# Another order of the wide stage's pairs, another list of PSUM banks, and the weights' quarters one pair later

## The chip, the cores and the metric

The kernel runs on one core of a Trainium2 chip. The metric is device time in microseconds (us). A core has a matrix engine (PE, with its weight load PEld), a vector engine (DVE), a scalar engine (ACT), a third elementwise engine (POOL) and SP, which here only issues transfers (DMAs). Every engine takes its own queue of instructions in order. A matmul writes to PSUM, eight banks of 128x512 fp32; DVE and ACT read PSUM and write on-chip memory. Engines wait for each other on semaphores.

## The reference

One layer of a trunk with two branches, for one sequence of 1024 rows of 1024, in fp32, with the RMS norm of the stream behind it:

```python
h = rms_norm(x, norm_w) * (1 + scale) + shift
gm_u, gm_v, gm_z, ssm_z, xbc, dt_raw, g_a, g_b = split(h @ w_in)
y_a = spatial_gating(gelu(gm_u), gelu(gm_v), ...) * silu(gm_z)      # W_s applied to layer_norm(v)
xbc = silu(causal_depthwise_conv(xbc, conv_w, conv_b))               # 4 taps
xs, bm, cm = split(xbc)
y_b = rms_norm((ssd_scan(xs, dt, a, bm, cm) + xs * d_skip) * silu(ssm_z))   # by groups
merged = sigmoid(g_a) * (y_a @ w_proj_a) + sigmoid(g_b) * (y_b @ w_proj_b)
return rms_norm(x + gate * (merged @ w_out), final_norm_w)
```

The product `h @ w_in` has 1024 x 1024 times 1024 x about 11,000; it is the "wide stage" of the kernel.

## The kernel before, in words

**Numbers.** fp32 values are split in a high and a low part (names end in `h` and `l`), and each product is made of three matmuls per tile: high x high, high x low, low x high.

**The wide stage.** The columns of `w_in` go in 41 pairs of two 128-column blocks. A pair is one call of `pair` (L594 on): seven products p1, p5, p6, p3, p2, p7, p4 of a Strassen-like scheme, each `product` (L580 on) being 12 matmuls of 128x512 into one bank (L588). The operands from the activations (`b11`, `t1` and so on) are made once; those from the weights are sums and differences of four loaded blocks `a11 a21 a22 a12` (DVE, L575 to L578), split into high parts by ACT (L536) and low parts by DVE (L537). The banks of a pair are `px` (p1, then p6 on top of it, later p7 and p4), and banks for p5 with p3 and for p2. In the profile these banks appear as `xNAME`, `yNAME`, `zNAME`, where NAME is the kind of pair: `cb` and `x` for the two kinds of convolution pairs, `uz` for a gated pair of z_g and u, `z`, `g` for the light ones, `v` for the first four. The evacuations stand in line L604: `c1NAME` is the first half of the pair's result and starts with ACT's copy of p1 before p6 is added to the same bank. So **p6 of a pair cannot start before ACT has copied p1**.

**What follows a pair.** A convolution pair has two results, each handled by `conv_done` (L912 on): ACT scales (L914), three DVE operations add the other taps (L916), ACT applies the silu (L918), and the result is stored to `s_d`. A light pair only needs ACT and a store. A gated pair g needs `mix(g)` (16 matmuls of 128x128 with the gating weights, then DVE), which reads `vn`, the normalized v; eight ACT operations (L879) write it once the statistics `vr` of v are there (L871) and v is loaded back as `vm`.

**Order of the work.** `jobs` (L934 to L961) is a list of pairs; the driver loop (L1316 on) makes the weights of pair n+1 while pair n runs. After each product `run_tasks()` issues what `later(delay, f)` has put `delay` products ahead: the statistics, `mix_load` and `mix` are placed so. From pair `NPRE` on, when the early pool `gx` is closed, the projection weights `w_proj_b` are prepared in 32 quarters, one every 4.3 products (`wb_quarter`, L820 on), and stored to `wb_d`. The instruction order of PE is as written; on ACT, DVE, POOL and SP a scheduler orders the instructions when the kernel is built.

**After the wide stage** come the SSD groups (`sl`, `dcy`, `yi`, `sp` and so on), with the first output projection `pma` between them. PSUM banks are handed out from a free list here (`bank` and `release`, L486 to L497) whose first order is `BANKS` (L146). Then the second projection is made by the same seven-product scheme (`multiply`, L1576 on, matmuls at L1584): its product p1 runs eight steps, the first of which writes the four banks `x0` to `x3`, which `places_of` (L1667) maps to physical banks. A bank is free once its last reader is done. In the last two groups of the SSD the row sums are in banks `pq6_1` and `pq7_1`; DVE copies them to the tiles `cwt` and `tri`, whose old content is no longer used.

Of the kernel before, what the change touches and what calls it, by code (L numbers as in the profile page):

```python
# [21 lines left out]
NG = 8  # L22
# [13 lines left out]
def hybrid_kernel(  # L36
# [24 lines left out]
    x, out = x[0], out[0]  # L61
# [42 lines left out]
    def store(dst, src):  # L104
        A.dma_start(dst, src)
# [37 lines left out]

    hpool = tc.tile_pool(name="hpool", bufs=1, reuse_waits="tile")
    hp = hpool.__enter__()
    BANKS = (1, 4, 3, 0, 2, 7, 5, 6)  # L146
    BN = ("b11", "t1", "t2", "b22", "t3", "b21", "t4")
    bop = {}
    for nm in BN:
# [26 lines left out]
    def wide(name, dt=F32):  # L176
        return w4[0].tile([P, S], dt, name=name, tag="w4", bufs=w4[1])
# [321 lines left out]
    def numbered(pool, c):  # L499
        for b in range(8):  # L500
            pool.tile([P, 512], F32, name=f"{c}{b}_0", tag=f"{c}{b}")
# [4 lines left out]
    def later(delay, f, *a):  # L506
        tasks.append((slot[0] + delay, f, a))

    def run_tasks():
        slot[0] += 1  # L510
        due = [t for t in tasks if t[0] <= slot[0]]
        for t in due:
            tasks.remove(t)
            t[1](*t[2])
# [79 lines left out]
    def pair(name, ops, done1, done2, after=None, whole=False):  # L594

        keep = pin if name in first_c1 and not p2r else lambda i: i
        after = after or (lambda n: None)  # L600

        def out(f, *a):
            with tc.high_priority():
                keep(f(*a))  # L604

        def p2():
            pz = bank(f"z{name}")
            product(pz, ops["p2"], "b21")
            out(V.tensor_add, c1[:, 0:512], c1[:, 0:512], pz)

        px = psum.tile([P, 512], F32, name=f"x{name}", tag="px", bufs=2)
        product(px, ops["p1"], "b11")
        c1 = first_c1.pop(name) if name in first_c1 else wide(f"c1{name}")
        out(A.copy, c1[:, 0:512], px)
        after(0)
        py = bank(f"y{name}")
        product(py, ops["p5"], "t1")
        c2 = wide(f"c2{name}") if p2r else None
        p5 = c2[:, 512:1024] if p2r else gm.tile([P, 512], F32, name=f"p5{name}", tag="p5")
        out(A.copy, p5, py)  # L620
        after(1)
        if pending:
            pending.pop()()
        product(px, ops["p6"], "t2", False)
        out(A.copy, c1[:, 512:1024], px)
        after(2)
        product(py, ops["p3"], "b22", False)
        out(V.tensor_add, c1[:, 512:1024], c1[:, 512:1024], py)
        after(3)
        if not whole:  # L630
            p2()
            after(4)
            done1(c1)
        product(px, ops["p7"], "t3", False)
        c2 = c2 or wide(f"c2{name}")
        out(V.tensor_add, c2[:, 512:1024], p5, px)
        after(4 if whole else 5)
        if whole:
            p2()
            done1(c1)  # L640

        def p4():
            product(px, ops["p4"], "t4", False)
            out(A.copy, c2[:, 0:512], px)
            done2(c2)

        if whole:
            p4()
        else:
            pending.append(p4)  # L650
# [156 lines left out]
    def wb_load(i):  # L807

        k, j = quarters[i]
        wbr[i] = raw = pre.tile([P, 4, P], F32, name=f"wbr{i}", tag="wbr", bufs=2)  # L810
        for k0, t in ((k, raw[:, 0:4:3]), (k + KT, raw[:, 1:3])):
            load(t, w_proj_b[k0 * P : (k0 + 1) * P, :].rearrange("p (b j c) -> p j b c", b=2, j=4)[:, j])
# [84 lines left out]
    def zg_done(g):  # L897
        def done(cz):
            A.activation(cz, cz, AF.Silu)
            V.tensor_mul(vns[g], cz, vns[g])  # L900
        return done

    def u_done(g):
        def done(cu):
            A.activation(cu, cu, AF.Gelu_apprx_tanh)
            V.tensor_mul(cu, cu, vns[g])
            store(ya_d[g], cu)
        return done
# [19 lines left out]
    def gate_done(i):  # L928
        def done(cg):
            A.activation(cg, cg, AF.Tanh, scale=0.5)  # L930
            store(th_d[i * P : (i + 1) * P, :], cg)
        return done

    def gcol(i):  # L934
        return (COL_GA if i < 8 else COL_GB) + (i % 8) * P

    jobs = []
    for g in range(0, NG, 2):
        jobs.append((f"v{g}", COL_V + g * P, COL_V + (g + 1) * P, v_done(g), v_done(g + 1), None))
    convs = []  # L940
# [5 lines left out]
    light = []  # L946
    for g in range(NG):
        light.append((f"z{g}", COL_Z + 2 * g * P, COL_Z + (2 * g + 1) * P, z_done(g, 0), z_done(g, 1), None))
    gpairs = []
    for i in range(2, 16, 2):  # L950
        gpairs.append((f"g{i}", gcol(i), gcol(i + 1), gate_done(i), gate_done(i + 1), None))
    for g in range(NG):
        jobs.append(convs.pop(0))
        jobs.append((f"uz{g}", COL_ZG + g * P, COL_U + g * P, zg_done(g), u_done(g), g))
    light = [p for q in zip(light, gpairs[:5] + [None] * 3) for p in q if p]
    while convs:
        jobs.append(convs.pop(0))
        for _ in range(1 if len(convs) in (1, 4, 7) else 2):
            jobs.append(light.pop(0))
    tail = gpairs[5:]  # L960


# [245 lines left out]
    def start_ssd():  # L1208
        fetch(2)
        done_d[0] = 2  # L1210
# [91 lines left out]
    def with_last(n, d):  # L1302
        def done(t):
            d(t)
            beside(n)
        return done

    todo = jobs + tail
    seconds, fold = [], []
    NPRE = 20  # L1310
    pre = None
    ops = pair_weights(*todo[0][:3], pinned=True)
    ps0.__exit__(None, None, None)
# [3 lines left out]
    for n, (name, _, _, d1, d2, g) in enumerate(todo):  # L1317
        if n == 4:
            later(7, stats)
        if n == NPRE:  # L1320
            gxpool.__exit__(None, None, None)
            prepool = tc.tile_pool(name="prepool", bufs=1, side="right", reuse_waits="tile")
            pre = prepool.__enter__()

            fold.append(pre.tile([P, NH], F32, name="fold", tag="fold"))
            wb_load(0)
            for i in range(len(quarters)):
                later(2 + 43 * i // 10, wb_quarter, i)
        if n == len(jobs):
            while tasks:  # L1330
                run_tasks()
            prepool.__exit__(None, None, None)
            gmpool.__exit__(None, None, None)
            w4pool.__exit__(None, None, None)
            p2rpool = tc.tile_pool(name="p2r", bufs=1, side="right", reuse_waits="tile")
            p2r = p2rpool.__enter__()
            w4[:] = [p2r, 4]
            first_c1[name] = wide(f"c1{name}")
        if 0 < n < len(todo) - 1:
            nxt = pair_weights(*todo[n + 1][:3])  # L1340
        if n + 2 == len(todo):
            wspool.__exit__(None, None, None)
            p2xpool = tc.tile_pool(name="p2x", bufs=1, side="right", reuse_waits="tile")
            p2x = p2xpool.__enter__()
            start_ssd()
        if g is not None:
            later(1 if g else 4, mix, g)
            if g + 1 < NG:
                later(7, mix_load, g + 1)
        if n + 1 == len(todo):  # L1350
            hand[0] = True
            pair(name, ops, with_last(5, d1), with_last(6, d2), beside, True)
        else:
            pair(name, ops, d1, d2, ops.get("after"), n in (3, len(jobs) - 1))
        ops = nxt if n else seconds[0]
# [56 lines left out]
    numbered(psum, "k")  # L1412
    free.extend(BANKS)
    for k in (6, 7):
# [249 lines left out]
    ps3 = tc.tile_pool(name="ps3", bufs=1, space=PSUM, reuse_waits="tile")  # L1664
    psb = ps3.__enter__()
    numbered(psb, "q")
    places_of = {"x": (1, 2, 3, 0), "y": range(4, 8)}  # L1667
    assert all(b > 3 for b in free[6:])
    wo, wor = {}, {}
    KO = (4, 5, 6, 7, 0, 1, 2, 3)  # L1670
# [90 lines left out]
    def inv_root(sq):  # L1761

        y, t, v = sq[:, 2:3], sq[:, 3:4], sq[:, 1:2]
        V.tensor_scalar(t, sq[:, 0:1], 1.0 / D, EPS, op0=ALU.mult, op1=ALU.add)
        V.tensor_scalar(y.bitcast(I32), t.bitcast(I32), -0.5, float(0x5F3759DF), op0=ALU.mult, op1=ALU.add)
        V.tensor_scalar_mul(v, t, -0.5)
        for _ in range(3):
            V.scalar_tensor_tensor(t, y, y, v, op0=ALU.mult, op1=ALU.mult)
            V.scalar_tensor_tensor(y, t, 1.5, y, op0=ALU.add, op1=ALU.mult)
        return y  # L1770
# [24 lines left out]
    for n, t in enumerate(tiles):  # L1795
# [22 lines left out]
        if last:  # L1818
            V.scalar_tensor_tensor(sq[:, 0:1], part[:, 0:1], part[:, 1:2], part[:, 2:3], op0=ALU.add, op1=ALU.add)
            y = inv_root(sq)  # L1820
# [4 lines left out]
        else:  # L1825
            V.tensor_add(r, pw, xr)
            A.activation(xr, r, AF.Square, accum_out=sq[:, 0:1])  # L1827
            y = inv_root(sq)
# [35 lines left out]
```

## Time and profile before

| | us |
|---|---|
| median of 3 runs | 1406.11 (1402.32 to 1409.07) |
| the profiled execution | 1407.12 |
| its span, first to last instruction | 1405.4 |
| mean granted clock of PE | 0.995 of full speed |
| wide stage, first `cb` product to last `g` pair's first product | 155.84 to 892.01 |
| second projection, first product | from 1155.61 |

The profiled execution lies 1.0 us above the median; about 1.7 us of it lie outside the span. The views used are the busy time of each engine, the list of waits (engine, what it was to compute, for whom it waited: us in total, times, longest), busy times by stretches of time, and the timeline, whose rows are start, duration, engine, line, operation, output and inputs, and at the end in brackets how long the engine was idle before, and what ended that.

### The profile page before, as it was taken

Reading aid. Unit: us, or ns where it says so; the run is one execution under the profiler, and the core shown is the slowest. Engines: PE = TensorE matmul, PEld = TensorE weight load, DVE = VectorE, ACT = ScalarE, POOL = GpSimd, SP = SyncE. Lnnn points to the kernel's source line nnn. Section 1 sums busy time; section 2 is a strip of 40 time slices with the busy share of each in tenths; the row PEclk is TensorE's granted clock in tenths of the full one; section 3 lists DMA queues with packets and bytes.
Section 4 is the critical chain, followed back from the end, with each engine's and each line's share of the span. In section 5 each row is a group of like instructions: output and inputs, shape, how many; then the busy total and the mean of one; then the engine's idle time right before and its main releaser. Section 6 shows DMA issues by size and latency. Waiting matters only on the chain.

```text
span 1405.4 us, 20414 instructions
## 1 busy us (share of the span) xinstructions
PE 1373.7 (98%) x7015; PEld 1132.1 (81%) x7015; DVE 1040.0 (74%) x1827; ACT 771.4 (55%) x1422; POOL 209.0 (15%) x198
## 2 busy tenths in 40 slices
PE   8999979999999999999999999999999999999997
PEld 6677868888888888888888888888888878888786
DVE  4677777667766898688788887478888768686743
ACT  6663466656666565555566555477786734233401
POOL 0000000000000000001010000017898870000000
PEclk9999989999999999999999999999999999999999
DMA  8555623332343576767676865488898849977432
GB/s 266 156 164 161 184 90 106 106 113 83 104 121 112 159 212 204 227 204 236 193 232 206 255 212 166 165 320 300 293 316 299 276 136 320 408 255 259 135 120 75
DMA packets 272043, 279.23 MB, mean 199 GB/s; under 512 B 18972, under 2 KB 224196, under 8 KB 271940
## 3 DMA queue, kind: packets, MB, share of 16 engines
q1 hardware_dynamic: 197956, 210.16, 47.8%
q10 hardware_dynamic: 73984, 67.78, 14.1%
q8 instruction: 55, 0.90, 0.3%
q14 instruction: 48, 0.39, 0.1%
HBM read 194.58 MB, written 83.30 MB: 198 GB/s over the span
## 4 chain that ended last, share of the span: by engine, by line
PE 80%; DVE 6%; DMA 6%; ACT 3%; issue 2%; SPq 2%; POOL 1%; POOLq 0%; ACTq 0%; DVEq 0%
PE xx L588 6%; PE xz L588 6%; PE xuz L588 6%; PE xg L588 5%; PE xcb L588 5%; PE pma L91 5%; PE yp L1584 5%; PE po L91 4%; PE x L1584 4%; PE yx L588 3%; PE yz L588 3%; PE yuz L588 3%; PE yg L588 3%; PE ycb L588 3%; PE yi L91 2%
## 5 line engine op out<-in xcount | busy, mean ns | idle before, releaser
L799 POOL TENSOR_TENSOR wog<-wog,gb 128x1024 f32<-128x1024 f32 x8 | 20.4, 2545 | 729.1 <-DVE wbr L835 535.5
L56 ACT ACTIVATE dcy<-dcy,nacs 128x128 f32<-128x128 f32 x256 | 78.4, 388 | 16.9 <-POOL dcy L56 16.4
L56 POOL TENSOR_SCALAR_AFFINE_SELECT dcy<-dcy 128x1024 f32<-128x1024 f32 x32 | 37.0, 1155 | 103.6 <-ACT ea L56 103.3
L918 ACT ACTIVATE ac<-ac 128x1024 f32<-128x1024 f32 x32 | 33.9, 1061 | 23.5 <-DVE ac L916 23.3
L56 ACT ACTIVATE ea<-dcy 64x512 f32<-64x512 f32 x64 | 40.3, 630 | 5.4 <-DMA dcy<-acs_d 5.0
L91 PE MATMUL pma<-yh,wah 128*128 128x512 f32 x128 | 43.0, 417 | 0.0
L91 PE MATMUL pma<-yh,wal 128*128 128x512 f32 x128 | 42.6, 414 | 0.0
L56 POOL TENSOR_TENSOR yz<-y,sl 128x512 f32<-128x512 f32 x32 | 41.3, 1291 | 0.6
L56 DVE TENSOR_TENSOR dcy<-dcy,pc 128x1024 f32<-128x1024 f32 x32 | 38.9, 1217 | 2.7 <-PE pc L94 1.8
L56 DVE TENSOR_TENSOR ym<-yn,ea 128x512 f32<-128x512 f32 (+1 forms) x32 | 19.9, 621 | 28.3 <-PE yn L91 28.1
L916 DVE SCALAR_TENSOR_TENSOR ac<-c2cb,cwt,ac 128x1023 f32<-128x1023 f32 (+2 forms) x24 | 30.6, 1275 | 13.1 <-ACT ac L914 12.9
L91 PE MATMUL pma<-yl,wah 128*128 128x512 f32 x128 | 39.9, 393 | 0.0
L56 POOL TENSOR_TENSOR y<-y,ym 128x512 f32<-128x512 f32 (+1 forms) x32 | 36.6, 1145 | 14.2 <-DVE ym L56 14.1
L916 DVE SCALAR_TENSOR_TENSOR ac<-c2x,cwt,ac 128x1023 f32<-128x1023 f32 (+2 forms) x24 | 31.8, 1325 | 8.6 <-ACT ac L914 7.1
L91 PE MATMUL yi<-dcy,xd 128*64 128x128 f32 x512 | 35.0, 279 | 3.2 <-DVE xe L56 2.9
L1827 ACT ACTIVATE xr<-r 128x1024 f32<-128x1024 f32 x7 | 7.4, 1061 | 53.2 <-issue 39.0
L1817 POOL TENSOR_TENSOR r<-r,fnw 128x256 f32<-128x256 f32 (+1 forms) x3 | 2.7, 916 | 220.5 <-ACT xr L1816 220.5
L91 PEld LDWEIGHTS yi<-dcy,xd 128*64 128x64 f32 x512 | 27.3, 136 | 9.5 <-issue 4.2
L91 PE MATMUL sp<-xe,bn 128*128 128x256 f32 x112 | 32.7, 409 | 0.0
L56 DVE SCALAR_TENSOR_TENSOR yn<-yn,par,rb 128x512 f32<-128x512 f32 x32 | 24.5, 766 | 9.6 <-DMA yn<-yb_d 9.6
L916 DVE SCALAR_TENSOR_TENSOR ac<-c1cb,cwt,ac 128x1023 f32<-128x1023 f32 (+2 forms) x24 | 30.6, 1277 | 0.7 <-ACT ac L914 0.7
L916 DVE SCALAR_TENSOR_TENSOR ac<-c1x,cwt,ac 128x1023 f32<-128x1023 f32 (+2 forms) x24 | 30.6, 1276 | 0.0
(2834 smaller groups left out, 4341.2 us busy)
## 6 DMA issues: line engine op xcount, KB each, us to landing
sl<-s_d SPq DMA_DIRECT2D x32, 768.0 KB
s_d<-ac ACTq DMA_DIRECT2D x32, 512.0 KB
dcy<-acs_d SPq DMA_DIRECT2D x32, 512.0 KB
aw<-in_ada_w_dram SPq DMA_DIRECT2D x16, 512.0 KB
wbr<-in_w_proj_b_dram SPq DMA_DIRECT2D x64, 128.0 KB
wb_d<-wbb ACTq DMA_DIRECT2D x32, 256.0 KB
wb_d<-wbc ACTq DMA_DIRECT2D x32, 256.0 KB
yb_d<-yz SPq DMA_DIRECT2D x32, 256.0 KB
```

The lines of the kernel that those rows point to most:

```text
L56: return lambda *a, **k: tc.keep_in_program_order(f(*a, **k))
L91: pin(PE.matmul(acc, l, r, start=first, stop=last))
L588: pin(PE.matmul(ps, lw[:, k * P : (k + 1) * P], r[k], start=first and n + k == 0, stop=n == 2 and k == 3, skip_group_check=not first))
L799: G.tensor_mul(w, w, gb)
L916: V.scalar_tensor_tensor(ac[:, s:], cc[:, : S - s], conv_wt[:, 3 - s, i : i + 1], ac[:, s:], op0=ALU.mult, op1=ALU.add)
L918: A.activation(ac, ac, AF.Silu)
L1584: pin(PE.matmul(ps[j], a[:, v, js], r, start=first and n + k == 0, stop=n == 2 and k == KT - 1, skip_group_check=not first))
L1817: G.tensor_mul(r[:, cs], r[:, cs], fnw[:, cs])
L1827: A.activation(xr, r, AF.Square, accum_out=sq[:, 0:1])
```

## The change

The pairs' order before (41 pairs; the seven products of each are the same in both):

```text
v0 v2 v4 v6 | cb0 uz0 x0 uz1 cb1 uz2 x1 uz3 cb2 uz4 x2 uz5 cb3 uz6 x3 uz7
| cb4 z0 x4 g2 z1 cb5 g4 z2 x5 g6 cb6 z3 g8 x6 z4 g10 cb7 z5 x7 z6 z7 | g12 g14
```

and after:

```text
v0 v2 v4 v6 | cb0 x0 uz0 cb1 uz1 x1 uz2 cb2 uz3 x2 uz4 cb3 uz5 x3 uz6 z0 uz7
| cb4 g2 x4 z1 g4 cb5 z2 x5 g6 z3 cb6 g8 x6 z4 g10 cb7 z5 x7 z6 z7 | g12 g14
```

Two convolution pairs stand between the v pairs and the first gated pair, the light pair z0 stands before the last gated one, and the light pairs among the rest move by a place. Besides, `mix(0)` comes three products after its pair's start in place of four, the quarters of `w_proj_b` start one pair later, and the order in which PSUM banks are first handed out, and the map of the second projection's x banks, are others.

```diff
-    BANKS = (1, 4, 3, 0, 2, 7, 5, 6)
+    BANKS = (1, 3, 5, 0, 6, 7, 2, 4)
...
+    light = [p for q in zip(light, gpairs[:5] + [None] * 3) for p in q if p]
     for g in range(NG):
-        jobs.append(convs.pop(0))
+        for _ in range(1 if g else 2):
+            jobs.append(convs.pop(0) if g < NG - 1 else light.pop(0))
         jobs.append((f"uz{g}", COL_ZG + g * P, COL_U + g * P, zg_done(g), u_done(g), g))
-    light = [p for q in zip(light, gpairs[:5] + [None] * 3) for p in q if p]
     while convs:
         jobs.append(convs.pop(0))
-        for _ in range(1 if len(convs) in (1, 4, 7) else 2):
+        for _ in range(1 if len(convs) in (1, 3, 5, 7) else 2):
             jobs.append(light.pop(0))
+    assert not light
...
-    NPRE = 20
+    NPRE = 21
...
-            later(1 if g else 4, mix, g)
+            later(1 if g else 3, mix, g)
...
-    places_of = {"x": (1, 2, 3, 0), "y": range(4, 8)}
+    places_of = {"x": (2, 1, 0, 3), "y": range(4, 8)}
```

**ACT at the sixth pair.** Names carry numbers of tiles; `waits` lists the semaphores on which the instruction waits. This is ACT's queue from the last evacuations of pair cb0 on, before:

```order
L604 COPY c2cb0_1850<-xcb0_1732 128x512 [waits DMAHW4_49,DMAHW7_49,PE_49,Pool_49]
L918 ACT_TABLE_LOAD [waits DVE_49]
L918 ACTIVATE ac24_1831<-ac24_1831 128x1024 [waits Activation_49]
L105 DMA s_d0_133<-ac24_1831 512x1x256 [waits Activation_49]
L879 ACTIVATE vn0_1933<-vm0_1928,vr_928 128x128 [waits DMAHW3_49,DMAHW4_49,DMAHW2_49,DMAHW5_49,DMAHW1_49,DMAHW7_49,DMAHW0_49,DVE_49]
L604 COPY c1uz0_1942<-xuz0_1895 128x512
L879 ACTIVATE vn0_1933<-vm0_1928,vr_928 128x128 x7
```

And now:

```order
L604 COPY c2cb0_1850<-xcb0_1732 128x512 [waits DMAHW4_49,DMAHW7_49,PE_49,Pool_49]
L918 ACT_TABLE_LOAD [waits DVE_49]
L918 ACTIVATE ac24_1831<-ac24_1831 128x1024 [waits Activation_49]
L105 DMA s_d0_133<-ac24_1831 512x1x256 [waits DMAHW2_49,Activation_49]
L879 ACTIVATE vn0_1933<-vm0_1928,vr_928 128x128 [waits DMAHW4_49,DMAHW3_49,DMAHW5_49,DMAHW1_49,DMAHW7_49,DMAHW0_49,DVE_49]
L604 COPY c1x0_1942<-xx0_1895 128x512
L879 ACTIVATE vn0_1933<-vm0_1928,vr_928 128x128 x7
```

The sixth pair is x0 where it was uz0; its copy of p1 has the same place in the queue.

**PE at the first step of the second projection.** The steps before it are the same in both. From the last matmul of `x1` on, before:

```order
L1584 MATMUL x1_11447<-p1bh0_11307,p1a0_11276 128x512
L1584 MATMUL x2_11448<-p1bh0_11307,p1a0_11276 128x512
L1584 MATMUL x2_11448<-p1bl0_11308,p1a0_11276 128x512
L1584 MATMUL x2_11448<-p1bh0_11307,p1a0_11276 128x512
L1584 MATMUL x3_11449<-p1bh0_11307,p1a0_11276 128x512 [waits DVE_49]
L1584 MATMUL x3_11449<-p1bl0_11308,p1a0_11276 128x512
```

And now (the lines are two further down in the file):

```order
L1586 MATMUL x1_11447<-p1bh0_11307,p1a0_11276 128x512
L1586 MATMUL x2_11448<-p1bh0_11307,p1a0_11276 128x512 [waits DVE_49]
L1586 MATMUL x2_11448<-p1bl0_11308,p1a0_11276 128x512
L1586 MATMUL x2_11448<-p1bh0_11307,p1a0_11276 128x512
L1586 MATMUL x3_11449<-p1bh0_11307,p1a0_11276 128x512 [waits DVE_49]
L1586 MATMUL x3_11449<-p1bl0_11308,p1a0_11276 128x512
```

Before, the bank of `x2` was last that of `sp7_3` and the bank of `x3` that of `pq6_1`, so that `x3` waited for DVE's copy `cwt<-pq6_1`. Now the bank of `x2` was that of `pq6_1`, and `x3` waits for DVE's copy `tri<-pq7_1`.

**DVE at the same place.** Its queue, the same in both:

```order
L56 TENSOR_SCALAR cwt_157<-pq6_1_11371 128x128 [waits PE_49]
L56 SCALAR_TENSOR_TENSOR yn4_0_11346<-yn4_0_11346,par2_156,rb4_0_11344 128x512 [waits DMAHW7_49,DMAHW0_49]
L56 TENSOR_TENSOR p1bl3_11394<-yn3_0_11334,p1bh3_11393 128x512 [waits Activation_49]
L56 TENSOR_TENSOR p1a3_11336<-p1r3_11337,p1a3_11336 128x512 [waits DMAHW5_49,Activation_49]
L56 TENSOR_SCALAR tri_151<-pq7_1_11400 128x128 [waits PE_49]
```

The two copies stand three operations apart, the first of which waits for a transfer.

## The prediction

> **What bounds the kernel now.** I read the page first: the span and the busy times.
>
> ```profile
> span 1405.4 us, 20414 instructions
> PE 1373.7 (98%) x7015; PEld 1132.1 (81%) x7015; DVE 1040.0 (74%) x1827; ACT 771.4 (55%) x1422; POOL 209.0 (15%) x198
> ```
>
> PE is busy for 1373.7 of 1405.4 us, so all that an edit of the order can win or lose is what PE waits for, and how fast it is clocked. The list of waits, PE's rows:
>
> ```profile
> PE xuz L588 <- ACT c1uz L604: 7.5, 1, 7.5
> ...
> PE pp L94 <- DMA pk<-in_ada_b_dram: 3.5, 1, 3.5
> ...
> PE yi L91 <- DVE xe L56: 2.9, 2, 1.5
> ...
> PE po L91 <- DVE r L1826: 1.0, 1, 1.0
> ```
>
> One wait of 7.5 us stands out, in the first gated pair, which the change moves. The others are small, and the 3.5 us lie in the start of the kernel, which is untouched. Next the timeline around the 7.5 us:
>
> ```profile
> 173.97 1.07 PE L588 MATMUL xuz<-b11h,p1uz0l 128*128 128x512 f32 x4
> ...
> 181.26 0.59 ACT L604 COPY c2cb<-xcb 128x512 f32<-128x512 f32 x1 [0.33 <-PE xcb L588]
> ...
> 183.04 1.27 DVE L916 SCALAR_TENSOR_TENSOR ac<-c1cb,cwt,ac 128x1021 f32<-128x1021 f32 x1
> ...
> 184.39 1.28 ACT L918 ACT_TABLE_LOAD   x1 [2.55 <-DVE vr L124]
> 185.69 1.06 ACT L918 ACTIVATE ac<-ac 128x1024 f32<-128x1024 f32 x1
> 186.11 0.17 DVE L871 SCALAR_TENSOR_TENSOR vr<-mv,vr 128x8 f32<-128x8 f32 x1
> 186.78 0.57 ACTq L105 DMA_DIRECT2D s_d<-ac  x1
> 187.68 0.49 ACT L879 ACTIVATE vn<-vm,vr 128x128 f32<-128x128 f32 x1 [0.93 <-ACT ac L918]
> 188.08 0.56 ACT L604 COPY c1uz<-xuz 128x512 f32<-128x512 f32 x1
> 188.69 2.08 PE L588 MATMUL xuz<-t2h,p6uz0h 128*128 128x512 f32 x4 [7.52 <-ACT c1uz L604]
> ```
>
> p1 of uz0 is complete at 175.04 (173.97 + 1.07), yet ACT copies it at 188.08 only. Ahead of the copy in ACT's queue stand the silu of cb0's first convolution (it idles 2.55 us until DVE's third tap ends at 183.04 + 1.27 = 184.31), its store, and the first `vn`, which needs `vr` (186.28). p6 starts 0.05 us after the copy's end (188.64). And it starts slowly; the stretch of the next twelve matmuls, in busy us of PE, PEld, DVE, ACT and POOL, then the granted clock, DMA share and GB/s:
>
> ```profile
> 188.69:194.18 5.49, 5.49 (x13) 4.33 (x14) 1.63 (x2) 4.41 (x9) 0.00 (x0) 0.50 0.42 127
> 200.00:927.40 727.40, 727.38 (x3273) 603.13 (x3272) 556.34 (x908) 430.56 (x707) 23.40 (x10) 1.00 0.56 171
> ```
>
> Twelve matmuls take 5.49 us at half clock, where the chain of waits has 2.72 us for them at full clock:
>
> ```profile
> 198.91 2.72 PE zuz L588 x12
> ```
>
> So this stall costs 7.52 + 2.77 = 10.3 us. From 200 to 927 us PE is busy for 727.38 of 727.40 us: there the order of the pairs has nothing to win, only something to lose.
>
> **The change part by part.** It neither adds nor removes an instruction on the engines; the terms are waits.
>
> *The stall at the sixth pair: 0.* The order printed above shows that ACT's queue there is the old one row for row: x0's copy stands where uz0's stood, behind the same silu, the same store and the same `vn`. DVE's queue up to there is the same too, but for the names. What sets 188.08 (the third tap, the silu, `vr`) is done for cb0 and v, which keep their places. So I expect p6 of x0 to start at 188.7, at half clock, and the 10.3 us to stay. Bounds of this term: -10.3 us if something in that chain comes early enough, and +2 if the store's or `vn`'s new semaphores are late; I take 0, since no row moved.
>
> *Two convolution pairs in a row: 0.* The work that the second one brings, by the rows of DVE:
>
> ```profile
> L916 DVE SCALAR_TENSOR_TENSOR ac<-c1x,cwt,ac 128x1023 f32<-128x1023 f32 (+2 forms) x24 | 30.6, 1276 | 0.0
> 204.08 0.69 DVE L578 TENSOR_TENSOR a21uz<-a11uz,a21uz 128x512 f32<-128x512 f32 x1
> ```
>
> Six taps at 1.28 us, 7.7; eleven sums and low parts of weights at 0.69, 7.6; three evacuations at 0.69, 2.1: 17.4 us, while a pair has 7 x 2.72 = 19.0 us of PE. It fits by 1.6 us, and the slack after the stall comes on top:
>
> ```profile
> 192.51 2.60 DVE L916 SCALAR_TENSOR_TENSOR ac<-c2cb,cwt,ac 128x1023 f32<-128x1023 f32 x2 [6.23 <-ACT ac L914]
> ```
>
> DVE has idled 6.23 us just then. The cover is this 6.23 + 1.6 = 7.8 us; what lies against it is what the gated pair spread out, at most one conv pair's six taps, 7.7. If the cover went, PE would wait for an evacuation, by 2 to 4 us (two or three taps in front of it).
>
> *The later pairs: 0.* Convolution and gated pairs alternate from there as before, one step on, and with the same rows on each engine. In the second half light pairs change places with light pairs; their DVE work is the weights alone. z0 ahead of uz7 takes the place of a convolution, which makes DVE lighter. `mix(0)`, 16 small matmuls, moves by one pair; it takes 1.78 us wherever it stands (seen at 226.11 for a later one), and `vn` is by then long done.
>
> ```profile
> 226.11 1.78 PE mix L91 x16
> ```
>
> *Quarters a pair later: 0.* Their last operation, and the first load that takes their space:
>
> ```profile
> 844.98 0.43 DVE L821 TENSOR_TENSOR wbc<-wbr,wbc 128x256 fp32r<-128x256 f32 x1 [1.34 <-ACT wbc L816]
> ...
> 883.70 0.34 SPq L100 DMA_DIRECT2D dcy<-acs_d  x1
> ```
>
> One pair is 19 us: the last one moves to about 864, and 19 us are left until 883.7. The load has to be later than that to cost anything.
>
> *The banks: +3.8.* In the SSD the new list gives other neighbours to the first `yi`, `sp` and `pma` banks; the rows on them show at most the 2.9 us of `yi`, which waits for `xe` and not for a bank: 0. At the first step of the second projection it is different. The timeline of PE and DVE there:
>
> ```profile
> 1155.61 0.39 PE L1584 MATMUL x<-p1bh,p1a 128*128 128x512 f32 x1
> ...
> 1157.42 0.62 PE L1584 MATMUL x<-p1bh,p1a 128*128 128x512 f32 x2
> ```
> ```profile
> 1157.08 0.28 DVE L56 TENSOR_SCALAR cwt<-pq 128x128 f32<-128x128 f32 x1
> 1159.26 0.75 DVE L56 SCALAR_TENSOR_TENSOR yn<-yn,par,rb 128x512 f32<-128x512 f32 x1 [1.90 <-DMA yn<-yb_d]
> 1159.93 0.69 DVE L56 TENSOR_TENSOR p1bl<-yn,p1bh 128x512 fp32r<-128x512 f32 x1
> 1160.54 0.68 DVE L56 TENSOR_TENSOR p1a<-p1r,p1a 128x512 fp32r<-128x512 f32 x1
> 1161.14 0.28 DVE L56 TENSOR_SCALAR tri<-pq 128x128 f32<-128x128 f32 x1
> ```
>
> A matmul steps by 2.72/12 = 0.227 us, so x2 begins six steps on, at 1156.97, and x3 nine steps on, at 1157.65. Before, x3 needed only `cwt<-pq`, done at 1157.36: no wait. Now x2 needs that one and begins at 1157.36 + 0.05 = 1157.41, 0.44 late; x3 would begin at 1158.09, but its bank was `pq7_1`, and the copy `tri<-pq` ends at 1161.14 + 0.28 = 1161.42. x3 begins at 1161.47, which is 1161.47 - 1157.65 = 3.8 us late. Behind it in PE's queue stands everything that follows, and PE does not wait again for more than 1.0 us up to the end, so the 3.8 us arrive there whole. Bounds: the copy is held up by `yn`, which waited 1.90 us for its load. With the load in time, `yn` follows the first copy and `tri` ends 1.90 us earlier, at 1159.52: 1.9 us late. With the load 2 us later than here (as far the other way), 5.8. I take the row's own value, since DVE's order is the same. This is the only term that is not nothing.
>
> **The sum.** 0 + 0 + 0 + 0 + 3.8 us on the profiled 1407.12 (1405.4 of span and 1.7 around it) gives 1410.9. The median of the runs shown is 1.0 below that execution: 1409.9. I predict **1410 us**; by the bounds of the last term alone 1408 to 1412.
>
> **The rivals.**
>
> *The new wait also halves the clock (slower).* x3 stands still from 1158.09 to 1161.47, 3.4 us without a matmul. The trace has two gaps to compare: after 7.52 us the clock was 0.50 for twelve matmuls, after 1.49 us nothing was lost, as 16 matmuls of `yi` in 1.09 us show:
>
> ```profile
> 1132.59 1.09 PE L91 MATMUL yi<-dcy,xd 128*64 128x128 f32 x16 [1.49 <-DVE xe L56]
> ```
>
> 3.4 lies between, nearer to the harmless one. If the clock falls, 2.77 more: 1406.1 + 3.8 + 2.8 = 1412.7; with the load 2 us later, 5.8 + 2.8, 1414.7. It decides for slower by over 0.5% (7.0 us, about what a measurement of this kernel can tell from no change) from a wait of 7.0 - 2.8 = 4.2 us on. The Trainium skill, "TensorE: Matmul & The Clock Gate", section "Part 1: The HAM clock gate", has the clock fall after one idle window of about 3.4 us that runs free of the program, which a gap of just that length would fill only by luck; that speaks for a small chance here, and the trace agrees with it at 7.52 and at 1.49 us.
>
> *The stall at 181 us goes.* If x0's copy got ahead of the silu, or p1 of x0 were taken early by other timing, 10.3 us would be won: 1406.1 - 10.3 + 3.8 = 1399.6. For it: the first gated pair no longer follows directly, and its first result is not needed so soon. Against it: ACT's rows have not changed places, and the row that ACT waits for is DVE's tap of cb0.
>
> *DVE falls behind with the second convolution.* 2 to 4 us more, and the 3.8: 1412 to 1414. For it: 7.8 us of cover against 7.7. Against it: half of the new pair's taps fall to the pair after, which has none of its own.
>
> *The new wait is hidden.* If `tri<-pq` ran ahead of PE, by the load coming early and PE late, or by another bound on PE before x0: 1406. Against it: even the early bound leaves 1.9 us.
>
> **How the numbers follow.** The forecast 0.52 (1408 to 1412), the clock 0.18 (1412.7 to 1414.7), the stall gone 0.08 (1399.6), DVE behind 0.10 (1412 to 1414), the wait hidden 0.12 (1406). The range from 1403 to 1416 holds the forecast, the slower cases and the hidden wait with a run's scatter of 3 us around the median; it leaves out the case at 1399.6. Slower by over 0.5% is over 1413.1: 0.14 of the clock's 0.18, half of DVE's, and 0.05 of the forecast for a late load: 0.24. Faster is under 1399.1: half of the third case, which lies at 1399.6, by the scatter, and 0.03 for a stall and a new wait both gone (1395.8): 0.07. Within 0.5%: 0.69.
>
> **What would show it.** Right: a PE wait of 7.5 us now named for x0's copy `c1x`, at the same 188.7, with 0.50 clock behind it; a wait of about 3.4 us at `x` L1586 for DVE's `tri`; else PE without gaps from 200 to 1155. Wrong: no gap at 181; a PE wait on an evacuation between 205 and 260; a gap at x3 that is not there, or that is followed by a clock of 0.50.

## The result, and the profile after

| | before | after |
|---|---|---|
| median, us | 1405.51 (5 runs) | 1425.55 (5 runs, 1424.17 to 1427.25) |
| ratio of the two | | 1.0146, 95% interval 1.0124 to 1.0169 |
| span of the profiled execution | 1405.4 | 1423.6 |

The changed kernel is 20 us slower. The prediction said 1410 and a range up to 1416. The page of the changed kernel:

```profile
span 1423.6 us, 20402 instructions
## 1 busy us (share of the span) xinstructions
PE 1380.6 (97%) x7015; PEld 1136.6 (80%) x7015; DVE 1046.7 (74%) x1827; ACT 772.4 (54%) x1422; POOL 210.0 (15%) x198
```

The same 7015 matmuls keep PE busy for 6.9 us longer (1380.6 against 1373.7), which is clock; the rest of the 18.2 us is waiting. PE's rows in its list of waits:

```profile
PE xx L588 <- ACT c1x L604: 7.5, 1, 7.5
PE px L94 <- ACT bn L56: 5.1, 1, 5.1
PE ycb L588 <- ACT p5cb L604: 3.8, 1, 3.8
...
PE x L1586 <- DVE tri L56: 3.5, 1, 3.5
...
PE xx L588 <- DVE c2x L604: 2.3, 2, 1.6
```

The first row is the old stall under its new name, as predicted. The fourth is the predicted wait at x3. The second, third and fifth were not predicted. A row that the kernel before has, `po` waiting 1.0 us for `r`, is gone. The granted clock behind four of the gaps, by stretches (length, then busy us of PE, PEld, DVE, ACT, POOL, the clock, DMA share, GB/s):

```profile
186.00:190.66 4.66, 4.66 (x11) 3.71 (x12) 0.85 (x1) 4.39 (x9) 0.00 (x0) 0.50 0.18 63
610.83:614.16 3.33, 3.33 (x8) 2.67 (x9) 3.04 (x4) 2.40 (x5) 0.00 (x0) 0.54 0.92 263
1134.39:1139.15 4.76, 4.76 (x32) 3.63 (x33) 1.87 (x3) 4.72 (x12) 3.57 (x4) 0.50 0.01 2
1174.47:1180.18 5.71, 5.71 (x13) 4.46 (x14) 3.75 (x6) 1.14 (x2) 0.00 (x0) 0.50 0.74 178
```

Each gap is followed by some us of half clock; between the start and the last matmuls, the kernel before has the first of these stretches alone. Where the time went is seen when the same matmul (by its number in PE's order) is looked up in both timelines and the times are subtracted:

| matmul | before | after | after less before |
|---|---|---|---|
| p6 of the sixth pair | 188.69 | 186.00 | -2.7 |
| first `yi` that waits for `xd` | 951.98 | 958.49 | +6.5 |
| `px` that waits for `bn` | 1122.79 | 1134.39 | +11.6 |
| x3's first | 1157.65 | 1174.47 | +16.8 |
| x, 13 matmuls on | 1160.59 | 1180.18 | +19.6 |
| `po`, near the end | 1331.69 | 1349.87 | +18.2 |

Of the -2.7, 2.0 come from the part ahead of the wide stage, which the change leaves alone, and the rest from the stretch up to the stall's end. From there the wide stage loses 9.2 us, the SSD 6.2 up to the second projection, x3 4.1 (0.3 of them at x2), and the half clock behind it 2.8; 1.4 come back in the last product, 1.0 of them the wait for `r` that is gone. Nothing is lost between 186 and 560 us: the steady alternation of convolution and gated pairs runs as before, and 0.5 us are won behind the stall. From 560 us on the wide stage therefore loses 9.7; the experiments below are compared by this stretch.

**The wide stage.** The timeline of ACT, SP and PE around the wait at 610 us:

```profile
598.85 0.82 SPq L100 DMA_DIRECT2D ag<-in_ada_w_dram  x2
599.72 0.43 SPq L100 DMA_DIRECT2D gb<-in_ada_b_dram  x1
...
600.06 0.45 ACTq L105 DMA_DIRECT2D wb_d<-wbb  x1
...
608.89 0.40 ACT L816 CAST wbb<-wbr 128x256 fp32r<-128x256 f32 x1 [5.45 <-DMA wb_d<-wbb]
...
610.19 0.58 ACT L604 COPY p5cb<-ycb 128x512 f32<-128x512 f32 x1 [0.38 <-DVE wbb L821]
...
610.83 2.08 PE L588 MATMUL ycb<-b22h,p3cb5h 128*128 128x512 f32 x4 [3.77 <-ACT p5cb L604]
```

Two loads `ag` of 512 KB each, the gate columns of `ada_w`, and one of `gb` are issued at 599 us, next to the stores of the quarters. The store issued at 600.06 frees its buffer at 608.89 only. ACT stands there with the next quarter's cast for 5.45 us, and behind it in ACT's queue stands the copy of p5 for which PE waits. These loads are placed by a count of products from the program's start (`later(145 + 14 * i, gate_part, ...)`, L1221), not by pairs: when pairs change places, the loads stay, and other pairs come to lie beside them. When they start also hangs on their buffers, which the results of the pairs use too (`wide`, L176). In the kernel before, the second load of this pair starts some 5 us after the first:

```profile
605.33 5.65 SPq L100 DMA_DIRECT2D ag<-in_ada_w_dram  x2
```

In the traces of all seven runs that have this wait, both loads start within 0.82 us beside cb5. That alone isn't enough: run 5 has them together at 593.12 us, and no such wait.

### The profile page after: what moved, and what is told of

Its sections match the earlier page's. It is cut to its first block, busy times and chain, and to the rows that moved or that the text cites. A ratio compares the mean times of both kernels' runs of the same rounds, so it can differ in the third digit from the quotient of the medians.

```text
span 1423.6 us, 20402 instructions
## 1 busy us (share of the span) xinstructions
PE 1380.6 (97%) x7015; PEld 1136.6 (80%) x7015; DVE 1046.7 (74%) x1827; ACT 772.4 (54%) x1422; POOL 210.0 (15%) x198
## 4 chain that ended last, share of the span: by engine, by line
PE 69%; DMA 10%; DVE 9%; issue 4%; ACT 3%; SPq 2%; POOL 2%; ACTq 0%; POOLq 0%; DVEq 0%
PE x L1586 6%; PE xuz L588 6%; PE po L91 6%; PE yp L1586 5%; PE xx L588 5%; PE xz L588 4%; PE xcb L588 4%; PE pma L91 3%; PE yuz L588 3%; PE xg L588 3%; PE yx L588 2%; PE ycb L588 2%; SPq L100 2%; PE xv L588 2%; PE yz L588 2%
## 5 line engine op out<-in xcount | busy, mean ns | idle before, releaser
L94 PE MATMUL px<-ident,sl 128*128 128x128 f32 x128 | 25.0, 278 | 5.1 <-ACT bn L56 5.1
```

Of the source, the lines that this page charges most:

```text
L94: pin(PE.transpose(dst, src, idn))
```

## The experiments

All were compared with runs of the kernel before on the same chip (medians 1404.5 to 1405.7 us). Differences between two runs are those of their medians; by the ratios they come out up to 1.5 us otherwise. The first four take the change apart: the banks, the quarters, the order. For the banks, the queues of DVE, ACT and SP are the same with either list, row for row.

**1. The change without its banks.**

```diff
-    BANKS = (1, 3, 5, 0, 6, 7, 2, 4)
+    BANKS = (1, 4, 3, 0, 2, 7, 5, 6)
-    places_of = {"x": (2, 1, 0, 3), "y": range(4, 8)}
+    places_of = {"x": (1, 2, 3, 0), "y": range(4, 8)}
```

> The change without its banks: the old list of banks and the old map of the x banks, everything else as changed; the queues of DVE, ACT and SP are those of the changed kernel row for row. Theory: the 3.5 us wait at x3 and the half clock behind it come from the banks alone, so 6.9 us go (3.8 of delay, 2.8 of half clock, 0.3 at x2) and the wide stage's 9.4 us stay: about 1418. If the 5.1 us wait of px for bn late in the SSD (4.4 us net) is of the banks too: about 1413. Rival, that a late transfer makes all of these: 1425, with the x3 wait still there.

Measured: 1418.02, ratio 1.0086 (1.0074 to 1.0098). The wait at x3 is gone; the wide stage's stays. But a new row stands among PE's waits:

```profile
PE ycb L588 <- ACT p5cb L604: 3.8, 1, 3.8
...
PE pma L91 <- DVE xe L56: 2.2, 1, 2.2
```

The kernel's text shows why: the wide stage hands out six banks in turn, the new order shifts this turn, and with the old list the bank of `pma` is the one of `px` of the same group, which DVE has not read yet (run 17 tests this). So the new list fits the new order in this place, and costs the wait at x3 in another.

**2. The banks alone**, on the kernel before.

> The kernel before with the new list of banks and the new x map alone; the queues of DVE, ACT and SP are those before, row for row. Theory: a wait of 3.5 us at x3 for tri, with half clock behind it, +6.9 us: about 1412. If the px wait for bn comes from the banks too, +11: 1416. Rival (the x3 wait needs the new order's timing): 1406.

Measured: 1410.15, ratio 1.0033 (1.0021 to 1.0045). The wait at x3 needs nothing but the banks:

```profile
PE x L1584 <- DVE tri L56: 3.3, 1, 3.3
```

It costs 4.5 us by the medians (3.0 to 6.3 by the interval); in the trace half clock stands behind it too.

**3. The quarters alone**, a pair later, on the kernel before: `NPRE = 21`.

> The kernel before with the quarters of w_proj_b a pair later (NPRE 21) and nothing else. Theory A, the quarters' new phase against pairs and gate loads makes the waits of the wide stage (ycb for p5cb at 611 us, xx for c2x at 563 and 863): PE waits of 4 to 7 us between 560 and 870, 1412 to 1416. Theory B, the order of the light pairs makes them: no PE wait over 0.5 us there, 1406.

Measured: 1407.86, ratio 1.0019 (1.0010 to 1.0029). PE's waits between 560 and 870 us are 1.6 us for `c2g` and others of 0.5 or less: less than theory A asked, more than B's nothing. By the numbered matmuls the stage loses 4.4 us from 560 us on; by the medians the run costs 2.2. A small cost.

**4. The change with the quarters undone**: `NPRE = 20`.

> The change with the quarters back at pair 20: new order, new banks. Theory A (the quarters' phase makes the wide stage's waits): the 9.4 us between 562 and 863 go, 1416. Theory B (the order of the light pairs): they stay, 1425. In both the x3 wait of 3.5 us stays.

Measured: 1417.58, ratio 1.0085 (1.0071 to 1.0098). That is 8.0 us below the changed kernel, about the time that theory A gave, and the wait for `p5cb` is gone: in this order the quarters' place is worth far more than the 2.2 us of run 3. In its trace the wide stage still loses 9.8 us, in other places (`c2z` 2.4, `p5g` 1.8, `c2x` 1.3), but the profiled execution, 1423.5, was the slowest of its five, about 6 us above the median, so its trace can't say what the others lose there. Theory A holds for the wait at `p5cb`; that the quarters make all that the stage loses is not shown.

**5. The places of the light pairs alone**, on the kernel before: `(1, 4, 7)` to `(1, 3, 5)`.

> The kernel before with one thing changed: single light pairs stand behind cb5, cb6 and cb7 as in the change (a 2 behind x4 and x5), and not behind cb4, x5 and cb7; the first half, the quarters and the banks are those before. Theory B1, the places of the light pairs in the second half make the waits: PE waits of 5 to 9 us between 560 and 870, 1411 to 1415. Theory B2, it is one light pair less in the second half (z0 gone ahead of uz7) or the phase of the gate loads, which are timed by slots: no such waits, 1406 to 1408.

Measured: 1405.19, ratio 1.0004 (0.9992 to 1.0015): nothing.

**6. The light pairs' places undone**, on the change without its banks: `(1, 3, 5, 7)` to `(0, 1, 4, 7)`.

> The change without its banks (1418.0 so far), with single light pairs behind cb4, x5, cb7 and x7, as close to the order before as 12 light pairs allow. Theory B1: the wide stage's waits of 9 to 12 us shrink to under 4 us, 1408 to 1411. Theory B2: they stay, about 1418.

Measured: 1419.02, ratio 1.0099 (1.0079 to 1.0120). The wait for `p5cb` stays at 3.9 us. With run 5, theory B1 falls from both sides: it isn't the places of the light pairs in the second half.

**7. The gate columns' loads 7 products later**, on the change without its banks.

```diff
-        later(145 + 14 * i, gate_part, [2 * i, 2 * i + 1])
+        later(152 + 14 * i, gate_part, [2 * i, 2 * i + 1])
```

> The change without its banks, with the loads of ada_w's gate columns (ag) 7 products later, by which they no longer fall on the stores of pair g4 and of two quarters at 600 us. Theory C, the 3.8 us wait of ycb for p5cb, with its half clock (5.6 us in all), is this collision: it goes, and 1412 to 1414 are left. Theory D, ACT is late there whatever the transfers: 1418.

Measured: 1411.17, ratio 1.0041 (1.0027 to 1.0056), 6.9 below run 1. The row for `p5cb` is gone. In the traces the wide stage loses 11.9 us from 560 us on in run 1 and 6.7 here, so 5.2 of the gain lie there; the edit also shifts the turn of the banks (see runs 14 and 15), and `pma` no longer waits for `xe`, but 1.3 us for `bn`. The largest wait left between 200 and 870 us:

```profile
PE xx L588 <- DVE c2x L604: 1.9, 2, 1.1
```

**8. The statistics of v later**, on the change without its banks: `later(7, stats)` to `later(12, stats)`.

> The change without its banks, with the statistics of v (and so the first vn) 12 products behind cb0's start in place of 7: x0's copy of p1 then stands ahead of cb0's silu and of vn in ACT's queue. Theory: the stall of 7.5 us at 180 us goes, with the half clock behind it: 10 us less, about 1408. Rival, the mix of uz0 then waits for vn: a wait of 2 to 6 us there, 1410 to 1414. Rival, the stall stays: 1418.

Measured: 1410.63, ratio 1.0034 (1.0018 to 1.0049), 7.4 below run 1, with a spread from 1404.5 to 1413.1. The first stall is gone. ACT's timeline there:

```profile
176.26 0.57 ACT L604 COPY c1x<-xx 128x512 f32<-128x512 f32 x1
...
183.28 1.28 ACT L918 ACT_TABLE_LOAD   x1 [2.54 <-DVE vr L124]
```

The copy of p1 comes 12 us earlier than the 188.08 of the kernel before, because the order that the scheduler builds now has it ahead of the silu. The first `mix`, which needs `vn`, is a pair later in the new order, as two convolutions lie between v and the first gated pair. That this is what made the room is argued and not shown: no run has the later statistics in the old order.

**9. Another map of the x banks**, on the changed kernel: x in banks 2, 1, 5, 0 and y in 4, 3, 6, 7.

> The changed kernel (1425.6) with one thing changed: the x banks of the second projection are 2, 1, 5, 0 and the y banks 4, 3, 6, 7, so that x3 waits for cwt again and no x bank for tri. Theory: the wait at x3 and the half clock behind it go, 6.9 us less, 1418.7; the wide stage's waits and the wait of px for bn stay. Rival, the time comes back later: 1422 or more.

Measured: 1429.14, ratio 1.0169 (1.0147 to 1.0190). A miss of the experiment's design: the time came back later, and with interest.

```profile
PE po L91 <- DVE tg L56: 13.0, 1, 13.0
```

The last product's first tile takes banks 4 and 5, and bank 5 now held an x bank, which is emptied at the very end of the second projection.

**10 and 11. All three mended, with that same map**, and the quarters at pair 21 and 20.

> The changed kernel with the x banks as in the run before, the statistics of v 12 products behind cb0's start, and the loads of ada_w's gate columns 7 products later. If the three costs are apart from each other: 1425.6 - 6.9 - 7.4 to 10 - 6.9 = 1402 to 1404, below the kernel before (1405). If the px wait for bn (4.4 us) goes with them: 1398 to 1400. Rival, another transfer is late in their place: 1408 or more.

> As the run before, with the quarters back at pair 20. If their phase against the gate loads is what counts, the earlier quarters meet the loads otherwise: by the run with the quarters undone (wide stage lost 9.8 us there, against 9.4) no difference beyond 2 us, 1400 to 1405.

Measured: 1415.00, ratio 1.0065 (1.0045 to 1.0085), and 1415.74, ratio 1.0067 (1.0047 to 1.0087). Both carry the same wait at `po` (12.4 and 12.8 us), so they tell nothing of the sum.

**12. A control: the gate loads 7 products later, on the kernel before.**

> The kernel before with the gate columns' loads 7 products later: a control. PE has no wait over 0.4 us there between 200 and 900 us, so by theory C there is nothing to gain: 1404 to 1407. If the move is a gain by itself (less traffic at a bad time everywhere): 1401 or less; if it makes a collision of its own: 1409 or more.

Measured: 1414.07, ratio 1.0052 (1.0033 to 1.0071): it makes a collision of its own, at the same pair cb5 and in the same form. From the timeline of that run:

```profile
580.06 0.82 SPq L100 DMA_DIRECT2D ag<-in_ada_w_dram  x2
...
581.35 0.64 ACTq L105 DMA_DIRECT2D wb_d<-wbb  x1
...
588.87 0.40 ACT L816 CAST wbb<-wbr 128x256 fp32r<-128x256 f32 x1 [3.82 <-DMA wb_d<-wbb]
...
590.17 0.58 ACT L604 COPY p5cb<-ycb 128x512 f32<-128x512 f32 x1 [0.38 <-DVE wbb L821]
```

Both loads start within 0.82 us here too. The move that heals one order harms the other. With runs 4 and 7 this shows that it is the place of the gate loads against the pairs and the quarters, and not the order as such, that makes the wait for `p5cb`: moving any of the three can make it or take it away.

**13. Banks that fit both places**, on the changed kernel.

```diff
-    BANKS = (1, 3, 5, 0, 6, 7, 2, 4)
+    BANKS = (1, 5, 3, 0, 6, 7, 2, 4)
-    places_of = {"x": (2, 1, 0, 3), "y": range(4, 8)}
+    places_of = {"x": (2, 1, 3, 0), "y": range(4, 8)}
```

> The changed kernel with banks 5 and 3 changed places in the list (1, 5, 3, 0, 6, 7, 2, 4) and x banks 2, 1, 3, 0: pq7_1 then lies in a y bank, x3 waits for cwt as before the change, and the x banks are 0 to 3 again, so that po4 finds its banks free as early as in the kernel before. Theory: 1425.6 less 6.9 (x3 and its half clock) is 1418.7, or 1414 if the px wait for bn goes as well; no PE wait over 1.5 us behind 1100 us. Rival, pma waits for a bank at 940 us (2.4 us): 1421.

Measured: 1417.10, ratio 1.0076 (1.0058 to 1.0095), 8.5 below the changed kernel. No wait for `tri`, none of `pma`; `px` waits 1.8 us for `bn`.

**14 and 15. This, with the statistics and the gate loads later**; quarters at pair 21 and 20.

> As the run before, with the statistics of v at 12 products and the gate columns' loads 7 products later. By e10 (1415.0) less its wait of po for tg (12.4 us and about 2.7 of half clock): 1400, 5 us below the kernel before. If the parts hide each other: 1405 or more.

> As the run before with the quarters at pair 20. By e11 (1415.7, its profiled execution 1410.5) less 15: 1395 to 1401.

Measured: 1402.65, ratio 0.9984 (0.9970 to 0.9998), and 1404.47, ratio 0.9998 (0.9986 to 1.0010). From run 13 to 14 it is 14.4 us; runs 7 and 8 gave 6.9 + 7.4 = 14.3 apart. Both edits work side by side, but that the sums agree so closely is luck: from 560 us on the wide stage wins 8.5 us from the trace of run 13 to that of run 14, where run 7 won 5.2, and run 14 loses 4.0 at a place where run 13 loses nothing. Run 15 is above the 1395 to 1401 that were expected. Both traces show `pma` waiting for `xe` again:

```profile
PE pma L91 <- DVE xe L56: 2.2, 1, 2.2
```

The gate's part has two banks of its own (`pg0`, `pg1`), so that moving it by a pair shifts the turn of six banks, and the list no longer fits.

**16. The gate loads 7 products earlier** than in the change, all else as in run 15.

> As e15 with the gate columns' loads 7 products earlier than in the change in place of 7 later. Theory C, that two of these loads beside cb5's first products make the wait of ycb for p5cb: at 138 they fall on the pairs ahead of cb5, and the wait is absent, 1395 to 1403. Rival, any place but 152 collides somewhere: a PE wait of 3 us or more between 540 and 680 us, 1404 to 1408.

Measured: 1407.17, ratio 1.0010 (0.9999 to 1.0021). The wait for `p5cb` is absent, as theory C asks, but there are others (`xg` for `c1g` 3.5 in two, the longer 2.4; `xz` for `c2z` 1.8). No single one reaches the 3 us that the rival asked, but the time is the rival's: an earlier place has waits of its own.

**17. A list that fits**, all else as in run 14: `BANKS = (1, 7, 3, 0, 6, 5, 2, 4)`.

> As e14 with banks 5 and 7 changed places in the list. In e14 and e15 pma's first second bank is the one that px1 of the first group had (moving the gate loads moves their two small products, and with them the ring of six banks of the wide stage, by a step), and PE waits 2.2 us there for xe, with half clock behind it. Now that bank was pc0's, read 5 us earlier. Theory: the wait and its half clock (3.6 us in e14's trace against the kernel before) go: 1399, 6 us below the kernel before. Rival, the wait only moves to yi or sp of the same group: 1402 to 1403.

Measured: **1398.94**, ratio 0.9959 (0.9943 to 0.9974), below both kernels. Its page, and PE's largest wait after the start (175 us on):

```profile
span 1395.6 us, 20423 instructions
...
PE 1370.9 (98%) x7015; PEld 1130.5 (81%) x7015; DVE 1044.6 (75%) x1827; ACT 772.5 (55%) x1422; POOL 208.8 (15%) x198
```
```profile
PE yi L91 <- DVE xe L56: 1.8, 2, 1.5
```

`pma` no longer waits for `xe`, 3.7 us by the medians. It is the changed kernel with three edits: this list with its x map, `later(152 + ...)`, and `later(12, stats)`.

## Why the prediction was wrong

**The stall at the sixth pair, 0: right.** It stayed at 7.5 us, as read from the order of ACT's queue. The rival in which it goes fell in the changed kernel; run 8 shows what it takes.

**Two convolutions in a row, 0: right.** No wait between 186 and 560 us.

**The later pairs, 0, and the quarters a pair later, 0: wrong, and this is the step that failed.** Each of the two was priced by itself. The text compared convolutions, gated and light pairs with each other, and took the light ones' work on DVE to be "the weights alone" (their evacuations stand there too, `c2g` L604 at 600.59 us for 0.68 us). It left out the work that runs on its own count of products: the gate columns' loads, whose place against the pairs and the quarters changed. And it looked at when the quarters' space is needed at the end, where indeed nothing waits, and not at what their stores meet on the way. In place of the two zeros the wide stage lost 9.2 us; the largest part is the wait for `p5cb`, 3.8 us with half clock behind it. In the new order, moving the loads gains 6.9 us by the medians (run 7), and putting the quarters back gains 8.0 (run 4); in the old order the quarters' move alone costs 2.2 (run 3). Both take the wait for `p5cb` away, so these gains don't add up: with the loads moved, the quarters' place is worth 1.8 us the other way (runs 14 and 15).

What the stage still loses from 560 us on is 3.9 us in run 17 and 6.7 in run 7, in waits of up to 1.9 us for evacuations; what makes these stays open. Run 5, which isn't slower than the kernel before by the medians, loses 3.7 there in its trace, so a part of this is scatter between executions. The loads `ag` stand in SP's rows of the profile before, and SP's and ACT's order beside cb5 was not compared row by row; only the steady part of the stage was.

**The banks, +3.8: the size of the wait right, its price too small.** x3 came 16.8 - 13.0 = 3.8 us later against x2, with DVE's rows as predicted:

```profile
1169.64 0.28 DVE L56 TENSOR_SCALAR cwt<-pq 128x128 f32<-128x128 f32 x1
1172.26 0.75 DVE L56 SCALAR_TENSOR_TENSOR yn<-yn,par,rb 128x512 f32<-128x512 f32 x1 [2.33 <-DMA yn<-yb_d]
...
1174.13 0.28 DVE L56 TENSOR_SCALAR tri<-pq 128x128 f32<-128x128 f32 x1
```

The rival with the half clock, given 0.18, is what happened: 2.8 us more. Calling a gap of 3.4 us nearer to the harmless one of 1.49 than to the one of 7.52 was the wrong reading, and the argument that such a gap would fill a whole window only by luck misled: about half a window was enough (see the last section). That the delay arrives at the end whole was wrong too: 1.4 us came back in the last product. Together the banks' term is 3.8 + 0.3 + 2.8 - 1.4 = 5.5 us in the trace, and 4.5 by the medians of run 2. In the same term, the banks at the SSD's start were read right: no new wait there in the changed kernel.

**The SSD, not foreseen.** About 4.4 us are the wait of `px` for `bn`, 5.1 against 0.8 before. ACT stands ahead of it in

```profile
1129.42 0.63 ACT L56 ACTIVATE yz<-yz 128x512 f32<-128x512 f32 x1 [7.41 <-DMA yb_d<-yz]
```

and waited there 6.17 us in the kernel before as well: a place on the edge, where a store that lands later at once costs PE. In the changed kernel's trace the transfers there come 1 to 2 us later against PE than before: the stores `yb_d` that start at 1096.10 before start at 1105.12, where PE is 7.2 us later. The wait was between 0.5 and 5.1 us over the runs without following any edit (3.5 in run 4, 1.8 in run 13, 0.6 in run 2), so what makes the transfers late stays open.

## What to carry to other kernels

When an order changes, list what does not move with it: tasks counted from the start, buffers that are handed out in turn, lists of banks. Each of them has a phase against the order, and the same edit heals one order and harms another (runs 7 and 12). Two such phases can't be priced one by one (runs 3 and 4). A bank list has to be looked at anew with each order (runs 1, 14 and 17), and the cheapest check is to write down, for each bank at the seam between two stages, who reads it last and when. The new order by itself left the stall at 7.5 us; the largest gain in run 17 is what was then moved in that order, the statistics (run 8, 7.4 us).

## What the runs showed of the hardware

Behind the start of the kernel, gaps of 3.1 us and more were followed by half clock every time. Shorter gaps differ. In run 14 a gap of 1.91 us was followed by nine matmuls at 0.53, in run 13 one of 1.86 us by twelve at full clock; in the changed kernel 1.62 us cost nothing but itself. From the two runs, in this order, the matmul behind the gap and the stretch that it begins:

```profile
653.31 1.88 PE L588 MATMUL xx<-t4h,p4x5h 128*128 128x512 f32 x4 [1.91 <-DVE c2x L604]
...
653.31:656.90 3.59, 3.59 (x9) 2.80 (x10) 3.59 (x7) 1.99 (x4) 0.00 (x0) 0.53 0.37 87
```
```profile
829.27 1.20 PE L588 MATMUL xcb<-t4h,p4cb7h 128*128 128x512 f32 x4 [1.86 <-DVE c2cb L604]
...
829.27:832.00 2.73, 2.73 (x12) 2.25 (x13) 2.73 (x5) 1.11 (x2) 0.00 (x0) 1.00 0.28 43
```

Length alone does not decide. The gap of 2.22 us at the same matmul, `pma` waiting for `xe`, cost half clock in runs 6, 14 and 15 and none in runs 1 and 8. Two matmuls behind it take 1.05 us in run 14 and 0.62 in run 1:

```profile
929.53 0.47 PE L91 MATMUL pma<-yh,wah 128*128 128x512 f32 x1 [2.23 <-DVE xe L56]
...
930.51 1.05 PE L91 MATMUL pma<-yh,wal 128*128 128x512 f32 x2
```
```profile
944.15 0.47 PE L91 MATMUL pma<-yh,wah 128*128 128x512 f32 x1 [2.22 <-DVE xe L56]
...
944.92 0.62 PE L91 MATMUL pma<-yh,wal 128*128 128x512 f32 x2
```

The moments at which the clock changes explain it. In the changed kernel it falls at 183.83, 610.50, 1132.74 and 1173.70 us: 0, 125, 278 and 290 steps of 3.413 us from the first. Such a grid runs through every trace, wherever the gaps lie, and the clock falls at the end of a step. In run 14 the whole gap at `pma` lies in one step; in run 1 the edge at 942.77 cuts it into 0.85 and 1.38 us. Over all traces, from the wide stage to the last product, every step in which PE idled for 1.91 us or more was followed by half clock, and none at full clock in which it idled for 1.73 or less; of five steps in between, one was. So about half of a step is enough, and the 3.53 us at x3, which put 2.75 into one step, could hardly have been harmless.

The Trainium skill, "TensorE: Matmul & The Clock Gate", section "Part 1: The HAM clock gate", has a window of about 3.4 us that runs free of the program, and half clock after at least one idle window. The grid of 3.413 us agrees with the free window; that a window must be idle altogether does not agree with the 1.91 us. So a gap from about 2 us on is to be priced with a chance of some 1.6 to 2.8 us of half clock, not with the gap alone: 1.6 is the nine matmuls of run 14 (3.59 us, where nine steps of 0.227 are 2.04), 2.8 the stretch behind x3.
